# A hybrid decoder trunk on one core: gate products of the linear attention issued ahead, the first blocks of the feed-forwards' second matrix three products later, five slots in the last feed-forward

## The chip, the cores and the metric

One core of a Trainium2 chip runs the whole program as one launch. The metric is the device time of that core in microseconds (us), taken as the median of several executions; the time before the change is 2344.31 us (three executions, 2343.51 to 2345.34). TensorE is the matrix engine; VectorE (DVE), ScalarE (ACT) and GpSimd (POOL) are the three engines for element-wise work; SyncE (SP) issues most DMAs.

## The reference

One inference step of a two-layer decoder for 512 prompt tokens and 8 x 4 sample tokens, 544 in all, with 1024 features. Each layer is feed-forward, mixer, feed-forward; the first layer's mixer is a gated linear attention, the second's an attention with forget gates.

```
h += 1/2 gate0 * SwiGLU(adaLN0(h));  h += gate1 * Mixer(adaLN1(h));  h += 1/2 gate2 * SwiGLU(adaLN2(h))

def swiglu(u, w_up, w_down):                 # 1024 -> 2 x 2816 -> 1024
    a, b = jnp.split(u @ w_up, 2, axis=-1)
    return (jax.nn.silu(a) * b) @ w_down

def gla_mixer(u, s0, w_in, w_gate2, b_gate, g_out, w_out):
    q, k, v, r, glr = jnp.split(u @ w_in, ...)            # 4 heads, keys 128, values 256 wide
    log_a = jax.nn.log_sigmoid(glr @ w_gate2 + b_gate) / 16
    o, S = gla_chunk_scan(q * 128 ** -0.5, k, v, log_a, s0)   # decay = exp(cumsum(log_a))
    return (rmsnorm(o, g_out) * jax.nn.silu(r)) @ w_out, S
```

Outputs are the new activations, the keys, values and forget values, and the recurrent states.

## The kernel before

Everything is kept feature-major: `h` and the input `u` of each product lie as 128 partitions x 8 blocks x 544 tokens. Each float32 product is made of three matrix products in a short format: an operand is split into a rounded part (`hi`, a cast on ScalarE) and the rest (`lo`, a subtraction on VectorE). `halves` does both, and line 157 (ScalarE) and line 158 (VectorE) are its two instructions; `acc3` (lines 176 to 178) does the three matrix products. The 544 tokens are worked on in two halves of 272 columns.

**Order.** The program text is a list by priority. A planner issues it: it goes through the text with its own estimate of each instruction's cost, and gives each engine the earliest instruction of the text that it takes to be ready. The result is one fixed queue for each engine; at run time an engine that waits for one instruction does not go past it. Tiles with the same tag share a few buffers; a tile's first writer waits until a buffer is free.

**Feed-forward (`ffn_seven`).** It is used four times, under the names 00, 02, 10 and 12. The 2816 middle features are 22 blocks, `q`. Blocks 0 to 2 are multiplied in the plain way (`plain_up`: 24 matmuls for each of two matrices and each half). From block 3 on, `seven` does the up-product with a seven-product scheme over the two halves of the depth and of the tokens: products 1, 2, 6, 7, 5, 4, 3, in this order, of 12 matmuls each. It needs sums of input blocks: `inputs` makes T1, T2 and T4 from uh and ul by additions and subtractions on VectorE (lines 549 and 556) followed by `halves`, and `last_input` writes T3 over a quarter of uh and ul that is read no more after the plain blocks. Product 7 reads T3. With `late=True` the two sums that T3 needs are made a second time in `last_input`; with `late=False` a tile `t3` of 4 x 272 numbers for each partition keeps them, and `last_input` is one cast and one subtraction, 1088 wide. `stage` makes the weights' sums of the next block (POOL, lines 649 to 656) and splits them.

The blocks are grouped into rounds, (0,1,2), (3,4,5), ..., (18 to 21). While the products of round r run, the second matrix is applied to round r-1: 16 down blocks (`down_block`; 8 output blocks x 2 halves, 9 matmuls each, then `residual` on VectorE, lines 408 and 411). `down_weights(r, m2)` loads and splits the weights for two output blocks (`rd`, then `hd` and `ld`, 768 wide). `between`, called after each product, decides how many down blocks are issued by then: 16 are spread evenly over `n = min(7 * len(round), 7 * (slots - 3))` products, where `slots` is the number of buffers for the middle features (`gh`, `gl`). With 6 slots n is 21, with 5 slots 14. 00 and 02 have `slots=5, late=True`, 10 has 6 slots and keeps `t3`, 12 has 6 slots and `late=True`. In 00 and 02 `between` also ticks off small products for the modulation vectors (`ada`); in 12 it ticks off the update of the sample states (`state_start`, then 16 `state_step`).

**Linear attention (`gla`).** After the first q and k features come the token-major products for v in three chunks (`proj_steps`; five units for each chunk: token tiles 0 and 1, the samples, token tiles 2 and 3). The chunk with the gate's input `glr` is first. Then `glr` is transposed to gT, and eight small products `z` (`gate_half`; four heads, two halves) are evaluated: `Abs` on ScalarE (line 1143) and a minimum on VectorE (line 1144). `gate_logs` does `Exp` and `Ln` over all heads at once (lines 1147 and 1148), and `gate_sums(hd)` a subtraction and a running sum for one head (lines 1151 and 1152). In the text the first three units of chunk `v0` stand before, among and behind the eight `gate_half`; the last two of them stand behind `gate_sums(0)`, and `ahead(5)` prepares the next weights. For each head, seven levels follow: differences of the running sum (lines 1213 and 1214), `Exp` (line 1215), products with q and k (lines 1216 and 1217), small matmuls `at` (line 1225), and evacuation. After each level `fill(FL[...])` issues so many units of the remaining q, k and r features.

## Time and profile before

| | |
|---|---|
| median of three executions | 2344.31 us |
| the profiled execution | 2349.15 us |
| its span, first to last instruction | 2347.4 us |
| granted TensorE clock, mean | 0.988 |
| feed-forward 00, from the first plain block to the end | about 31 to 447 us |
| linear attention | about 440 to 735 us |
| feed-forward 02 | about 735 to 1165 us |
| feed-forward 10 | about 1281 to 1655 us |
| feed-forward 12 | about 1950 to 2347 us |

The profiled execution is 4.84 us above the median, of which 1.75 us lie outside its span. In the rows of a timeline the columns are: start and length in us, engine, line, operation, what is written from what, shape and number of instructions, and in brackets how long the engine had been idle and for whom it waited. In the list of waits the columns are: total in us, how often, and the longest.

### The profile page before, as it was taken

The numbers are of one execution on the slowest core, as the hardware profiler recorded it, in microseconds if no ns is written. First come the engines' busy times: TensorE is split into PE (matmuls) and PEld (weight loads), VectorE is DVE, ScalarE is ACT, GpSimd is POOL, SyncE is SP. The second block draws the span as 40 slices with busy tenths as digits, with TensorE's granted clock in tenths as the row PEclk, the third lists the DMA queues.
The fourth block names the chain that finished last, engine by engine and source line by source line (L and its number), as shares of the span: only waits on it lengthen the run. The fifth ranks groups of instructions, "written<-read, shape, count | busy, mean of one in ns | idle before, by whom it ended". The sixth has DMA issues, their size and how long they took to land.

```text
span 2347.4 us, 48948 instructions
## 1 busy us (share of the span) xinstructions
PE 2279.5 (97%) x19292; PEld 2128.8 (91%) x19292; DVE 1743.9 (74%) x3796; ACT 978.6 (42%) x1818; POOL 897.7 (38%) x908
## 2 busy tenths in 40 slices
PE   7999999998989999999999999999998999999999
PEld 6899999997979999999879999999895589999999
DVE  6877667738555976777685977787948758979885
ACT  3343333434533443333334444444446544434432
POOL 0344544206202354554210455652325122555551
PEclk8999999999999999999999999999999999999999
DMA  8545555422253426555448233333256641334441
GB/s 307 182 126 189 192 196 186 120 62 65 61 181 97 137 89 196 172 191 182 162 127 242 79 97 91 105 89 97 69 115 199 185 137 44 97 91 130 141 144 70
DMA packets 363035, 319.43 MB, mean 136 GB/s; under 512 B 25247, under 2 KB 326141, under 8 KB 362758
## 3 DMA queue, kind: packets, MB, share of 16 engines
q1 hardware_dynamic: 350182, 308.63, 41.8%
q0 software_dynamic: 12624, 7.67, 1.7%
q8 instruction: 152, 2.49, 0.4%
q14 instruction: 77, 0.63, 0.1%
HBM read 298.17 MB, written 18.38 MB: 135 GB/s over the span
## 4 chain that ended last, share of the span: by engine, by line
PE 80%; DVE 11%; DMA 3%; ACT 2%; issue 1%; POOL 1%; SPq 1%; DVEq 0%; ACTq 0%; POOLq 0%
PE p L176 11%; PE p L178 11%; PE p L177 11%; PE pd L177 7%; PE pd L178 7%; PE pd L176 7%; PE ada L242 2%; DVE nv L382 1%; DVE x L556 1%; PE fo L1835 1%; DVE lu L158 1%; PE pT L1820 1%; DVE ul L402 1%; PE fg L176 1%; PE fg L178 1%
## 5 line engine op out<-in xcount | busy, mean ns | idle before, releaser
L178 PE MATMUL pd<-gh,ld 128*128 128x272 f32 x1408 | 406.2, 288 | 4.3 <-DVE ld L158 4.3
L176 PE MATMUL pd<-gh,hd 128*128 128x272 f32 x1408 | 406.7, 289 | 3.3 <-DVE u L681 2.0
L177 PE MATMUL pd<-gl,hd 128*128 128x272 f32 x1408 | 406.3, 289 | 1.2 <-DVE gl L158 0.7
L176 PE MATMUL p<-uh,hu 128*128 128x272 f32 x1216 | 351.5, 289 | 0.0
L178 PE MATMUL p<-uh,lu 128*128 128x272 f32 x1216 | 350.7, 288 | 0.0
L177 PE MATMUL p<-ul,hu 128*128 128x272 f32 x1216 | 350.3, 288 | 0.0
L178 PEld LDWEIGHTS pd<-gh,ld 128*128 128x128 f32 x1408 | 265.6, 189 | 4.9 <-DVE ld L158 4.9
L176 PEld LDWEIGHTS pd<-gh,hd 128*128 128x128 f32 x1408 | 265.6, 189 | 4.2 <-DVE u L681 2.2
L177 PEld LDWEIGHTS pd<-gl,hd 128*128 128x128 f32 x1408 | 265.6, 189 | 2.2 <-DVE gl L158 0.9
L176 PE MATMUL p<-th,hu 128*128 128x272 f32 x912 | 264.9, 291 | 0.0
L178 PE MATMUL p<-th,lu 128*128 128x272 f32 x912 | 264.2, 290 | 0.0
L177 PE MATMUL p<-tl,hu 128*128 128x272 f32 x912 | 263.6, 289 | 0.0
L408 DVE SCALAR_TENSOR_TENSOR h<-pd,mods,h 128x272 f32<-128x272 f32 (+1 forms) x448 | 212.0, 477 | 65.9 <-PE pd L178 64.2
L158 DVE TENSOR_TENSOR lu<-rua,hu 128x512 fp32r<-128x512 f32 (+1 forms) x228 | 232.3, 1019 | 36.0 <-ACT hu L157 33.0
L157 ACT CAST hu<-rua 128x512 fp32r<-128x512 f32 (+1 forms) x228 | 173.8, 762 | 175.9 <-PE p L177 103.9
L176 PEld LDWEIGHTS p<-uh,hu 128*128 128x128 f32 x1216 | 229.0, 188 | 5.5 <-issue 2.9
L649 POOL TENSOR_TENSOR s<-rua,rub 128x512 f32<-128x512 f32 x76 | 121.5, 1599 | 290.9 <-DMA rub<-in_w_ffn_up_dram 161.7
L177 PEld LDWEIGHTS p<-ul,hu 128*128 128x128 f32 x1216 | 229.2, 189 | 0.1
L178 PEld LDWEIGHTS p<-uh,lu 128*128 128x128 f32 x1216 | 228.9, 188 | 0.0
L413 POOL TENSOR_TENSOR h<-h,gs 128x32 f32<-128x32 f32 x224 | 114.9, 513 | 239.4 <-DVE gs L411 223.3
L655 POOL TENSOR_TENSOR rua<-rub,rua 128x512 f32<-128x512 f32 x76 | 109.4, 1439 | 183.1 <-DVE lu L158 101.6
L176 PEld LDWEIGHTS p<-th,hu 128*128 128x128 f32 x912 | 172.7, 189 | 4.9 <-issue 2.1
(541 smaller groups left out, 5938.5 us busy)
## 6 DMA issues: line engine op xcount, KB each, us to landing
adaw<-in_w_ada_dram SPq DMA_DIRECT2D x128, 512.0 KB, 6.0
rua<-in_w_ffn_up_dram SPq DMA_DIRECT2D x88, 512.0 KB, 4.3
rub<-in_w_ffn_up_dram SPq DMA_DIRECT2D x88, 512.0 KB, 3.8
rd<-in_w_ffn_down_dram SPq DMA_DIRECT2D x96, 384.0 KB, 3.3
adah<-in_w_ada_dram SPq DMA_DIRECT2D x16, 512.0 KB, 5.9
adaw<-in_w_ada_kv_dram SPq DMA_DIRECT2D x16, 512.0 KB, 6.7
rd<-in_w_ffn_down_dram SPq DMA_DIRECT2D x16, 512.0 KB, 3.5
kp<-in_cache_k_dram SPq DMA_DIRECT2D x16, 512.0 KB, 10.7
```

Of the source, the lines that this page charges most:

```text
L157: S.copy(hi, src)
L158: V.tensor_tensor(out=lo, in0=src, in1=hi.bitcast(F32), op=ALU.subtract)
L176: PE.matmul(ps, lhsT=wh, rhs=xh, start=first and i == 0, stop=False)
L177: PE.matmul(ps, lhsT=wh, rhs=xl, start=False, stop=False)
L178: PE.matmul(ps, lhsT=wl, rhs=xh, start=False, stop=last and i == n - 1)
L242: PE.matmul(ps[32 * j:32 * j + 32, 0:256], lhsT=sc[:, k, :], rhs=t[:, j * 256:(j + 1) * 256], start=k == 0, stop=k == NB - 1)
L382: V.scalar_tensor_tensor(out=v[:, 0:p1 - t0], in0=h[:, k, t0:p1], scalar=mods[:, scale + k, 0:1], in1=rb[:, t0:p1], op0=ALU.mult, op1=ALU. ...
L402: V.scalar_tensor_tensor(out=ul[:, k, t0:p1], in0=v[:, :n], scalar=mods[:, shift + k, 0:1], in1=uh[:, k, t0:p1].bitcast(F32), op0=ALU.add, ...
L408: V.scalar_tensor_tensor(out=h[:, m, t0:p1], in0=ps[:, 0:n], scalar=mods[:, gate + m, 0:1], in1=h[:, m, t0:p1], op0=ALU.mult, op1=ALU.add)
L413: G.tensor_tensor(out=h[:, m, TP:T], in0=h[:, m, TP:T], in1=st[:], op=ALU.add)
L649: G.tensor_tensor(out=o["s3"][:], in0=a11, in1=a21, op=ALU.subtract)
L655: G.tensor_tensor(out=a11, in0=a21, in1=a11, op=ALU.subtract)
```

## The change

Three edits. In the linear attention all eight `gate_half` stand ahead of the units of `v0`; the logarithms are computed for head 0 and for heads 1 to 3 in separate instructions; three units of `v0` follow `gate_sums(0)`, and the last two are issued after the first and the second level of head 0, where `ahead(5)` now stands too; the row of `FL` for head 0 keeps its four units and has them later. In the feed-forwards the counter of `between` starts at -3 in the first round (`LAG`), so that the 16 down blocks of blocks 0 to 2 start three products later and are spread over three fewer; their first weights are loaded and split after the second product instead of ahead of the first. In the last feed-forward (12) `late=True` is taken away and there are five slots.

```diff
-FL = [1, 0, 1, 0, 1, 0, 1] + [0, 1, 0, 1, 0, 1, 1] * 3
+FL = [0, 0, 1, 1, 0, 1, 1] + [0, 1, 0, 1, 0, 1, 1] * 3
+LAG = 3
...
-            down_weights(0, 0)
             load(plain + 1)
             for r in range(1, len(rounds)):
                 todo = blocks(r - 1)
-                n, done, gone = min(7 * len(rounds[r]), 7 * (slots - 3)), [0], [0]
+                n, done, gone = min(7 * len(rounds[r]), 7 * (slots - 3)), [0 if r > 1 else -LAG], [0]
+                if r == 1:
+                    n -= LAG
                 def between():
                     done[0] += 1
+                    if r == 1 and done[0] == 2 - LAG:
+                        down_weights(0, 0)
                     while gone[0] < min(2 * NB * done[0] // n, 2 * NB):
...
-                S.activation(e1, e1, AF.Exp, scale=-1.0)
-                S.activation(e1, e1, AF.Ln, bias=1.0)
+                for func, scale, bias in ((AF.Exp, -1.0, 0.0), (AF.Ln, 1.0, 1.0)):
+                    for e in (e1[:, 0:1], e1[:, 1:4]):
+                        S.activation(e, e, func, scale=scale, bias=bias)
...
-            zs = [(hd, half) for hd in range(4) for half in range(2)]
-            for i in range(3):
-                v0[i]()
-                for _ in range((3, 3, 2)[i]):
-                    gate_half(*zs.pop(0))
+            for hd in range(4):
+                for half in range(2):
+                    gate_half(hd, half)
             gate_logs()
             gate_sums(0)
-            for s_ in v0[3:]:
+            for s_ in v0[:3]:
                 s_()
-            ahead(5)
+            v0 = v0[3:]
...
+                    if v0:
+                        v0.pop(0)()
+                        if not v0:
+                            ahead(5)
                     fill(FL[7 * hd + li])
...
-                  final=True, late=True)
+                  final=True, slots=5)
```

## The prediction

> **What bounds the kernel now.** I read the page's busy times first, then the list of TensorE's waits, then the timelines around the longest of them.

> ```profile
> PE 2279.5 (97%) x19292; PEld 2128.8 (91%) x19292; DVE 1743.9 (74%) x3796; ACT 978.6 (42%) x1818; POOL 897.7 (38%) x908
> ...
> PE at L1225 <- POOL xb L1217: 6.1, 3, 4.2
> ...
> PE pd L178 <- DVE ld L158: 4.3, 3, 2.4
> ```

> TensorE is busy 97% of the span, so an edit that keeps the matmuls can only gain idle time of TensorE, and slow matmuls. The longest waits touched by the edits are those for line 1217 (linear attention) and for `ld`, the split of the second matrix. The timeline of TensorE shows each with its place; I take the feed-forwards first (00, 02, 12 in this order).

> ```profile
> 85.83 0.39 PE L178 MATMUL pd<-gh,ld 128*128 128x272 f32 x1 [1.38 <-DVE ld L158]
> ...
> 90.57 0.39 PE L176 MATMUL pd<-gh,hd 128*128 128x272 f32 x1 [1.33 <-ACT gh L157]
> 91.70 0.59 PE L177 MATMUL pd<-gl,hd 128*128 128x272 f32 x1 [0.73 <-DVE gl L158]
> ...
> 799.15 0.39 PE L178 MATMUL pd<-gh,ld 128*128 128x272 f32 x1 [0.48 <-DVE ld L158]
> ...
> 2000.07 0.60 PE L178 MATMUL pd<-gh,ld 128*128 128x272 f32 x1 [2.40 <-DVE ld L158]
> 2000.46 0.43 PE L176 MATMUL pd<-gh,hd 128*128 128x272 f32 x1
> 2000.69 0.43 PE L177 MATMUL pd<-gl,hd 128*128 128x272 f32 x1
> ...
> 2127.24 0.39 PE L176 MATMUL pd<-gh,hd 128*128 128x272 f32 x1 [1.97 <-DVE u L681]
> ```

> The first down blocks wait 1.38 + 1.33 + 0.73 = 3.44 us in 00, 0.48 in 02 and 2.40 in 12; in 10 nothing waits there. After the 2.40 the matmuls start 0.23 us apart. In the linear attention:

> ```profile
> 528.58 0.29 PE L176 MATMUL gq<-uh,hgq 128*128 128x272 f32 x1
> ...
> 531.97 0.29 PE L176 MATMUL gq<-uh,hgq 128*128 128x272 f32 x1
> 532.09 0.29 PE L177 MATMUL gq<-ul,hgq 128*128 128x272 f32 x1
> 536.53 1.12 PE L1225 MATMUL at<-xb 128*64 128x64 f32 x8 [4.16 <-POOL xb L1217]
> ...
> 538.20 0.43 PE L177 MATMUL gq<-ul,hgq 128*128 128x272 f32 x1
> 538.43 0.43 PE L178 MATMUL gq<-uh,lgq 128*128 128x272 f32 x1
> ```

> v0 is done at 528.58, where the first q feature starts. The first `at` then stands at the head of TensorE's queue for 4.16 us. Matmuls of the same shape start 0.12 us apart ahead of it and 0.23 behind it, for about 15 of them: 15 x 0.11 = 1.6 us more. In 12 some 12 slow ones behind the 2.40 make 1.3 us.

> [...]

> **The change, part by part.**

> *Gate products ahead.* What the first `at` waits for is a chain over four engines.

> ```profile
> 510.27 1.18 PE L1142 MATMUL z<-kk,w 16*128 16x272 f32 x4
> ...
> 512.38 0.72 PE L1142 MATMUL z<-kk,w 16*128 16x272 f32 x2
> ...
> 507.28 0.18 DVE L1135 COPY kk<-glrT 16x32 f32<-16x32 f32 x1 [0.17 <-PE glrT L1134]
> ...
> 520.42 0.95 ACT L1143 ACTIVATE rr<-z,vec 128x272 f32<-128x272 f32 x2 [1.05 <-PE z L1142]
> ...
> 522.68 2.02 ACT L1147 ACTIVATE rr<-rr 128x2176 f32<-128x2176 f32 x1
> 524.60 1.03 ACT L157 CAST hgq<-rgq 128x1024 fp32r<-128x1024 f32 x1
> ...
> 526.95 2.03 ACT L1148 ACTIVATE rr<-rr 128x2176 f32<-128x2176 f32 x1
> ...
> 529.00 1.36 DVE L1151 TENSOR_TENSOR rr<-rr 128x544 f32<-128x544 f32 x2 [2.11 <-ACT rr L1148]
> 530.28 2.47 DVE L1152 TENSOR_TENSOR_SCAN bb<-kk,rr 128x544 f32<-128x544 f32 x2
> ```

> gT is complete at 507.28 + 0.18 = 507.5, and yet the last Abs ends at 520.42 + 0.95 = 521.4, since the products stand between units of v0. Issued first, a pair follows a pair after 512.38 - 510.27 = 2.1 us (two buffers, each freed by Abs and minimum): four pairs start at 507.5, 509.6, 511.7 and 513.8, and the last Abs ends some 1.7 later, at 515.5. From the last Abs to the first `at` it is 536.53 - 521.4 = 15.1 us now. Of these go: the cast `hgq` (1.03), which stands between Exp and Ln and moves behind v0; the second head's subtraction and scan (1.36/2 + 2.47/2 = 1.9), which the queue has between head 0's scan and its levels and which now wait for the second Ln; and Ln over four heads, of which only head 0 is left on the chain. No row has a 544-wide Exp or Ln. A line through 0.475 us for 272 columns (the Abs) and 2.02 for 2176 gives 0.70 for 544 and 1.58 for 1632; so Exp, Exp, Ln cost 2.98 where 4.05 stood, 1.1 less, and the two added instructions cost ScalarE about 0.5, half of it off the chain. 15.1 - 1.0 - 1.9 - 1.1 = 11.1: `at` is ready at 526.6. v0 keeps TensorE busy until 528.6. The work covers the chain by 2 us, and the four feature units stay for the later levels.

> So 4.16 + 1.6 = 5.8 can go. I book 4.7, since the last two units are behind the first two levels in priority, and the planner may put `at` ahead of matmuls that were ready: 1.1 stay. Bounds: all 5.8 and the smaller level waits too, 6.1 - 4.2 = 1.9 by the list's row (7.7 together); against the change, `at` in the queue directly behind v0's third unit, which would end near 521 (two units of 24 matmuls, 0.12 x 352/272 = 0.16 us each, sooner than 528.6): 526.6 - 521 = 5.6 of waiting instead of 4.16, a loss of 1.5.

> What is moved along: `ahead(5)` and its DMA come some units later. Its weights are first read after the third level, and its `hi` and `lo` buffers come free with v0's last unit; if the cast (1.03) and split come late, the first q feature waits for about 2 us that `at` work would then cover only in part. That lies within the 1.1 kept back and the bounds.

> *Down blocks three products later.* TensorE's matmuls are the same. What follows product 2 is now product 6 and product 7, with block 0 as the fifth thing instead of the second. So product 7, with T3, is wanted up to three blocks (27 matmuls of 0.125 us = 3.4 us) sooner, and the first `ld` three products (36 matmuls, 4.5 us) later. VectorE decides:

> ```profile
> 85.69 2.98 DVE L158 TENSOR_TENSOR ul<-x,uh 128x272 fp32r<-128x272 f32 x2
> ...
> 90.34 0.94 DVE L158 TENSOR_TENSOR ld<-rd,hd 128x768 fp32r<-128x768 f32 x1
> ...
> 92.83 0.44 DVE L158 TENSOR_TENSOR ul<-x,uh 128x272 fp32r<-128x272 f32 x1
> ...
> 803.41 0.43 DVE L158 TENSOR_TENSOR ul<-x,uh 128x272 fp32r<-128x272 f32 x1
> ...
> 1320.94 1.29 DVE L549 TENSOR_TENSOR ul<-t,uh 128x1088 fp32r<-128x1088 f32 x1 [0.33 <-ACT uh L582]
> ...
> 1972.99 1.14 DVE L556 TENSOR_TENSOR x<-uh,ul 128x272 f32<-128x272 f32 x3
> ...
> 1998.00 2.02 DVE L158 TENSOR_TENSOR ld<-rd,hd 128x768 fp32r<-128x768 f32 x1
> ...
> 2005.71 0.77 DVE L158 TENSOR_TENSOR ul<-x,uh 128x272 fp32r<-128x272 f32 x1
> ```

> In 00 T3 is complete at 92.83 + 0.44 = 93.3. Two `ld` (0.94 each) and a residual that stood before it go behind it: 90.9. Product 1 and two block matmuls had ended at 85.83 - 1.38 = 84.45, so product 7 comes at 84.2 + 2 x 1.5 = 87.2 and reads its last part of T3 at 88.3: a wait of 2.6 instead of 3.44. Then `ld` is split while product 7 runs. I book 0.7, between 3.44 (all of it; the planner puts product 5, which needs no T3, in between) and -1.0 (`ld` late too). In 02 T3 ends at 803.84, less the same two splits 801.0 to 802.0, and product 7 reads its last part at 802.5: in time. I book 0.4 of 0.48, with -0.8 for an `ld` that is late. In 10 TensorE waits for nothing there; the slack that shrinks by 3.4 us costs, I take, 0.2 (0 to 0.5). The second edge is SP's queue: `rd` now goes behind the next block's two loads, and takes a later buffer; the loads are 10 us ahead of their use, and I book nothing.

> That 16 blocks come in 11 products (00, 02, 12) or 18 (10): each block costs VectorE less than it costs TensorE (9 x 0.125 = 1.1 us), so a denser mixture leaves it no later. Nothing booked.

> *`t3` in 12.* Twelve additions and subtractions (1.14/3 = 0.38 each) go and four stay: -3.0; four `ul` (0.43) become one of 1.29: -0.4. T3 was complete at 2005.71 + 0.77 = 2006.5; less 3.4 and less `ld` (2.02) it is 2001.1. Product 2 had ended at 2000.07 - 2.40 - 0.25 = 1997.4; product 6 ends at 1998.9 and product 7 reads its last part at 2000.0: a wait of 1.1 to 1.2 in place of 2.40. A wait of that length has no slow matmuls behind it (85.83), so 1.2 + 1.3 = 2.5 booked, between 0 and 3.7.

> *Five slots in 12.* All 16 blocks of a round stand in 14 of its 21 products, and seven run alone.

> ```profile
> 944.00:956.00 12.00, 12.00 (x113) 10.91 (x112) 10.40 (x17) 4.77 (x9) 9.66 (x8) 1.00 0.62 215
> ...
> 2148.00:2160.00 12.00, 12.00 (x98) 12.00 (x98) 11.80 (x20) 5.24 (x10) 10.08 (x10) 1.00 0.57 171
> ```

> These are 12 us of 02 (five slots, no down block) and of 12 with state steps: VectorE works 10.40 and 11.80 of them (fifth column) and TensorE does not wait. Together they would be more than full, so I book 0.4 of loss, between 0 and 3. The 1.97 at 2127.24 falls in the state's start; its place among blocks changes, and I leave it, with 2 either way.

> **Sum** against the profiled execution of 2349.15: -4.7 - 0.7 - 0.4 + 0.2 - 2.5 + 0.4 = -7.7, so 2341.4; that execution stands 4.84 above the median, and 2344.31 - 7.7 = 2336.6.

> **The rivals.**

> *Everything goes.* All waits named vanish with the smaller ones: 7.7 + 3.44 + 0.48 + 3.7 + 1.97 = 17.3, so 2327.0; half of what I hold back gives about 2332. For it: the waits are single ones.

> *The queue freezes the wait.* The planner set `at` 4 us too early; if it errs by the same amount in the new order, the 5.8 stay with ready matmuls behind them. -7.7 + 4.7 = -3.0: 2341.3. For it: ready q matmuls stood behind the waiting `at` at 536.53 already. Against: a chain without the second head's scan.

> *VectorE and POOL.* Two `ul` took 2.98 where others take 0.44 each; the next block's POOL sums, whose loads are no longer behind `rd`, can fall on T3's steps. A freeze of 2.1 in each of 00, 02 and 12 takes what was booked there (3.6): 2340.2. [...]

> *Slower: five slots.* In the seven products alone (10.5 us) VectorE needs 10.5 x 10.40/12 = 9.1 at least, 11.80/12 of it or more with state steps. If one freeze of 2.1 and 1.5 of overload fall in each of four rounds and reach TensorE, that is 14.4: 2336.2 + 14.4 = 2350.6. It decides from about 13 us on. Against: five PSUM banks stand between the two engines.

> **How the numbers follow.** 0.2% (4.7 us) is about what a measurement here can tell. Chances: my sum 0.44 (its own range 2333 to 2339.5), everything goes 0.12, frozen queue 0.22, VectorE and POOL 0.14, five slots 0.08. Faster takes the first two and 0.10 of the next two, near the edge at 2339.6: 0.66. Same 0.27, slower 0.07. The range 2330 to 2343.5 leaves out the ends of the first rival and of the last.

> **What the profile would show.** Right: no wait over 1.5 us at line 1225 with v0's matmuls running up to it, the Abs rows done by 516; `at` first near 527; no `ld` wait in 12; T3 in 12 complete some 5 us sooner than now, counted from product 1. Wrong: an `at` wait of 4 us with gv matmuls behind it; product 7 waiting for `ul` or `uh`; new waits on VectorE every 50 us in the last feed-forward.

## Result: slower, and the profile after

The changed kernel takes 2360.57 us (median of five executions, 2355.89 to 2365.09) against 2343.51 for the kernel before in the same comparison: a ratio of 1.0071, 95% interval 1.0054 to 1.0089. I had forecast 2336.6, a gain. The profiled execution took 2365.09 (span 2363.3).

The page's busy times and the list of TensorE's waits (in us: total, times, longest) of the changed kernel:

```profile
PE 2291.6 (97%) x19292; PEld 2136.9 (90%) x19292; DVE 1742.8 (74%) x3785; ACT 978.7 (41%) x1819; POOL 900.7 (38%) x908
```

```profile
PE p L177 <- ACT uh L158: 6.5, 4, 2.1
...
PE pd L177 <- ACT gh L687: 4.1, 3, 2.3
...
PE p L178 <- DVE ul L159: 2.8, 5, 1.1
...
PE pd L178 <- POOL gl L688: 1.8, 3, 0.9
...
PE p L178 <- DVE tl L159: 1.6, 1, 1.6
```

The 6.1 us of `at` and the 4.3 of `pd` waiting for `ld` are gone from the list. In their place products (`p`) wait for `uh` and `ul`, which is T3, and in one place for `tl`, the last part of T2; down blocks (`pd`) wait for `gh` and `gl`. TensorE's timeline gives the places: product 7 in 00 and in 02, product 6 (`tl`) and product 7 (`ul`) in 12, then two of the seams in 12, the places where one round ends and the next begins.

```profile
88.68 0.40 PE L178 MATMUL p<-ul,hu 128*128 128x272 f32 x1 [1.10 <-DVE ul L159]
90.12 0.40 PE L178 MATMUL p<-ul,hu 128*128 128x272 f32 x1 [0.79 <-DVE ul L159]
92.69 0.60 PE L177 MATMUL p<-uh,hu 128*128 128x272 f32 x1 [2.06 <-ACT uh L158]
95.32 0.59 PE L177 MATMUL p<-uh,hu 128*128 128x272 f32 x1 [1.20 <-ACT uh L158]
...
801.28 0.39 PE L177 MATMUL p<-uh,hu 128*128 128x272 f32 x1 [1.72 <-ACT uh L158]
...
2006.17 0.48 PE L178 MATMUL p<-tl,hu 128*128 128x272 f32 x1 [1.59 <-DVE tl L159]
2008.07 0.59 PE L178 MATMUL p<-ul,hu 128*128 128x272 f32 x1 [0.97 <-DVE ul L550]
...
2160.97 0.39 PE L177 MATMUL pd<-gh,hd 128*128 128x272 f32 x1 [2.32 <-ACT gh L687]
...
2267.81 0.39 PE L177 MATMUL pd<-gh,hd 128*128 128x272 f32 x1 [1.52 <-ACT gh L687]
2269.10 0.58 PE L178 MATMUL pd<-gl,hd 128*128 128x272 f32 x1 [0.90 <-POOL gl L688]
```

To see what each place cost, waits, slow matmuls and all, I compare where the same matmul starts in the profile of a kernel and in the profile before. The difference of two such shifts, at the two ends of a stretch, is what the stretch lost (+) or gained (-). In the table, "booked" is the prediction, "after" the changed kernel, and the other columns are runs described below. The points in brackets are times of the kernel before, chosen where both have done the same blocks.

| Stretch | booked | after | gates alone | later blocks alone | slots and T3 alone |
|---|---|---|---|---|---|
| 00, first round (82 to 138) | -0.7 | +4.4 | -0.2 | +4.0 | -1.4 |
| linear attention (505 to 620) | -4.7 | -8.4 | -8.7 | -1.2 | -1.6 |
| 02, first round (766 to 837) | -0.4 | +5.9 | +0.1 | +6.4 | 0.0 |
| 10, first round (1305 to 1384) | +0.2 | +0.3 | +0.3 | +1.2 | +0.3 |
| 12, first round (1994 to 2048) | -2.5 | +1.4 | 0.0 | +3.5 | -2.1 |
| 12, rounds 2 and 3 (2048 to 2150) | 0 | -1.3 | 0.0 | 0.0 | -1.4 |
| 12, round 4 to the end (2150 to 2326) | +0.4 | +10.2 | 0.0 | -0.2 | +9.5 |

The seven stretches give +12.5 of the 15.9 us between the two profiles; the other 3.4 us lie outside them, where no edit reaches directly. There, too, a stretch differs by up to about 2 us from one profile to another: -2.1 to +1.2 in the linear attention, over the kernels without the gate edit. In the first round of 00, six of the nine kernels that leave it as it was show -1.4 to -1.6 and three -0.2 to 0.0.

So the gates gained more than booked, and two things that were booked at next to nothing (a gain of 0.9 for the later blocks, a loss of 0.4 for five slots) lost some 25 us between them: 15 by the later blocks alone, 9.5 to 10 by five slots. What made T3 late in 00 is in VectorE's and GpSimd's timelines:

```profile
84.27 1.42 DVE L550 TENSOR_TENSOR x<-x,x 128x272 f32<-128x272 f32 x1
85.72 1.42 DVE L557 TENSOR_TENSOR x<-uh,ul 128x272 f32<-128x272 f32 x1
87.06 1.21 DVE L159 TENSOR_TENSOR lu<-rua,hu 128x1024 fp32r<-128x1024 f32 x1
88.20 1.86 DVE L159 TENSOR_TENSOR ul<-x,uh 128x272 fp32r<-128x272 f32 x2
89.98 1.50 DVE L557 TENSOR_TENSOR x<-uh,ul 128x272 f32<-128x272 f32 x1
...
93.52 0.95 DVE L159 TENSOR_TENSOR ld<-rd,hd 128x768 fp32r<-128x768 f32 x1
...
94.74 0.43 DVE L682 TENSOR_TENSOR a<-p,u 128x272 f32<-128x272 f32 x1
95.09 0.68 DVE L159 TENSOR_TENSOR lu<-s,hu 128x512 fp32r<-128x512 f32 x1
95.69 0.43 DVE L159 TENSOR_TENSOR ul<-x,uh 128x272 fp32r<-128x272 f32 x1
```

```profile
81.95 3.44 POOL L650 TENSOR_TENSOR s<-rua,rub 128x512 f32<-128x512 f32 x1 [5.66 <-DVE g L623]
85.47 1.37 POOL L651 TENSOR_TENSOR rub<-rub 128x512 f32<-128x512 f32 x1
88.41 1.35 POOL L656 TENSOR_TENSOR rua<-rub,rua 128x512 f32<-128x512 f32 x1 [1.57 <-issue]
89.84 1.35 POOL L657 TENSOR_TENSOR rua<-rua 128x512 f32<-128x512 f32 x1
```

T3 is complete at 95.69 + 0.43 = 96.1. The third row is the split of the *next* block's weights (`stage` step 1); it now stands ahead of T3's last steps, and the sums at lines 656 and 657, which wait for it, run beside them. In the kernel before, the same split came behind T3 (complete at 93.3):

```profile
93.78 1.23 DVE L158 TENSOR_TENSOR lu<-rua,hu 128x1024 fp32r<-128x1024 f32 x1 [0.16 <-ACT hu L157]
```

Operations of 0.43 us take 1.42 to 1.50 while GpSimd adds. The first two slow `x` run beside the sums at lines 650 and 651 (step 0), which now come 3 us sooner (81.95 instead of 84.91); the load of one of their inputs is issued at 73.4 instead of 81.1, since it now goes ahead of `rd`. Product 7 waits 5.4 us for T3 in all (with one more wait of 0.26), where I had forecast 2.6.

### The profile page after: what moved, and what is told of

It is laid out like the page before. It is cut to its first block, busy times and chain, and to the rows that moved or that the text cites. A ratio compares the mean times of both kernels' runs of the same rounds, so it can differ in the third digit from the quotient of the medians.

```text
span 2363.3 us, 48925 instructions
## 1 busy us (share of the span) xinstructions
PE 2291.6 (97%) x19292; PEld 2136.9 (90%) x19292; DVE 1742.8 (74%) x3785; ACT 978.7 (41%) x1819; POOL 900.7 (38%) x908
## 4 chain that ended last, share of the span: by engine, by line
PE 77%; DVE 13%; DMA 4%; ACT 2%; issue 2%; POOL 2%; SPq 1%; ACTq 0%; DVEq 0%; POOLq 0%
PE p L177 11%; PE p L178 10%; PE p L179 10%; PE pd L178 7%; PE pd L177 7%; PE pd L179 7%; PE ada L243 2%; DVE lu L159 2%; DVE x L557 1%; DVE x L550 1%; DMA kp<-in_cache_k_dram 1%; DVE nv L383 1%; PE fo L1843 1%; DVE tl L159 1%; PE pT L1828 1%
## 5 line engine op out<-in xcount | busy, mean ns | idle before, releaser
L177 PE MATMUL pd<-gh,hd 128*128 128x272 f32 x1408 | 408.4, 290 | 4.1 <-ACT gh L687 4.1
L178 PE MATMUL pd<-gl,hd 128*128 128x272 f32 x1408 | 407.4, 289 | 1.9 <-POOL gl L688 1.8
L177 PE MATMUL p<-uh,hu 128*128 128x272 f32 x1216 | 353.3, 291 | 6.5 <-ACT uh L158 6.5
L178 PE MATMUL p<-ul,hu 128*128 128x272 f32 x1216 | 353.0, 290 | 4.1 <-DVE ul L159 2.8
L177 PEld LDWEIGHTS pd<-gh,hd 128*128 128x128 f32 x1408 | 267.1, 190 | 5.1 <-ACT gh L687 4.7
L178 PEld LDWEIGHTS pd<-gl,hd 128*128 128x128 f32 x1408 | 267.1, 190 | 3.0 <-POOL gl L688 2.7
L177 PE MATMUL p<-th,hu 128*128 128x272 f32 x912 | 265.3, 291 | 0.8 <-DVE gs L412 0.8
L178 PE MATMUL p<-tl,hu 128*128 128x272 f32 x912 | 263.5, 289 | 1.6 <-DVE tl L159 1.6
L158 ACT CAST hu<-rua 128x512 fp32r<-128x512 f32 (+1 forms) x228 | 173.8, 762 | 195.8 <-PE p L178 128.2
L177 PEld LDWEIGHTS p<-uh,hu 128*128 128x128 f32 x1216 | 230.6, 190 | 12.8 <-ACT uh L158 7.5
L178 PEld LDWEIGHTS p<-ul,hu 128*128 128x128 f32 x1216 | 230.7, 190 | 6.1 <-DVE ul L159 4.3
L177 PEld LDWEIGHTS p<-th,hu 128*128 128x128 f32 x912 | 172.9, 190 | 6.1 <-issue 2.5
```

Of the source, the lines that this page charges most:

```text
L158: S.copy(hi, src)
L177: PE.matmul(ps, lhsT=wh, rhs=xh, start=first and i == 0, stop=False)
L178: PE.matmul(ps, lhsT=wh, rhs=xl, start=False, stop=False)
```

## The experiments

All times are medians; each ratio is against the kernel before in the same comparison (its median was 2345.3 to 2345.9), with its 95% interval. The ratio is not the quotient of the two medians, and where the executions lie unevenly the two differ.

**The three edits by themselves.**

Gates alone (the hunks of the change's diff in `FL` and `gla`):

> The gate edit alone (all eight gate products first, logarithms in two parts, v0's last two units inside head 0), on the kernel before. Theory (the parts add up): TensorE reaches the first feature of the output projection 8 us sooner, since the 4.16 us wait for the first `at`, its slow matmuls and the small level waits are filled by v0's units: 2335.5, between 2333 and 2338. Rival (the gain seen in the linear attention of the changed kernel belongs partly to the 4 us by which it was late there): 2340 or more.

Measured 2339.16, ratio 0.9972 (0.9957 to 0.9986): a clear gain. The time is 1.2 us above the expected range and below the rival's 2340; the kernel before was slower, too, in this comparison (2345.67 instead of 2344.31), and the ratio applied to 2344.31 gives 2337.7, at the upper edge of the range. The later blocks alone (the hunks with `LAG` and `down_weights`):

> The later first blocks alone (counter from -3 in the first round of each feed-forward, first weights after product 2), on the kernel before. Theory (T3 is late): product 7 is wanted up to three blocks sooner and waits for the four last casts and subtractions of T3 in 00, 02 and 12; about +4.5 in 00, +6 in 02, +1 in 10 and +4 in 12, where T3 still is made the long way: 2359, between 2354 and 2363. Rival (the loss at the starts comes from the second matrix's weights or from the 11-product packing): the waits in the list are for `ld` or stand at blocks, and not at product 7.

Measured 2359.34, ratio 1.0056 (1.0035 to 1.0077), as expected. Five slots and the T3 tile alone (the last hunk, `late=True` to `slots=5`):

> The last edit alone (feed-forward 12 with t3 and five slots), on the kernel before. Theory (seams): the first block of a round follows product 1 instead of product 2, straight after seven products in which VectorE and POOL are full, and waits for the last middle block's gh and gl; about 9 us lost over rounds 3 to 6, 2 to 3 gained at the start of 12 through t3 and 1.5 at the state's start: 2348, between 2345 and 2352. Rival (the loss in 12 comes from the later first blocks, and five slots are harmless): 2339 to 2342.

Measured 2350.6, ratio 1.0021 (1.0008 to 1.0033), as expected. The parts add up to +0.5%, against +0.71% together; the intervals allow that. The table above shows the same by place.

**Why T3 is late.** In the first block of the seven-product scheme, steps 1 and 2 of the next block's staging are issued behind product 5 (with `LAG = 3`, nothing else changed):

```diff
                 a0 = plus_ps(q, "a0", ...)
-                stage(q + 1, 1)
+                if q != plain: stage(q + 1, 1)
...
-                stage(q + 1, 2)                 # behind product 7
+                if q != plain: stage(q + 1, 2)
...
                 u4 = plus_ps(q, "a4", p5, u2)
+                if q == plain: stage(q + 1, 1); stage(q + 1, 2)
```

> The later down blocks alone, with one more edit: in the first product block after the plain ones, steps 1 and 2 of the next block's staging are issued behind product 5 instead of behind products 2 and 7, which in the queue puts lu of that block (1.21 us on VectorE) and the two POOL sums that wait for it behind the last part of T3. Theory A (T3 is late because the next block's staging and the POOL sums behind it were queued ahead of its last parts; they cost lu 1.21 and two freezes of 1.1 in each of the feed-forwards 00, 02 and 12): 2349 to 2353, 6 to 10 us under the 2359.3 of the later blocks alone, with product 7's waits in 00 down from 5.4 to about 2.6. Rival B (product 7 is simply wanted 3.4 us sooner than T3 can be there; the staging fills time that is free): 2356 or more.

Measured 2352.65, ratio 1.0029 (1.0014 to 1.0043): inside theory A's range, 6.7 us less than the later blocks alone, and product 7's waits in 00 are 3.0 us instead of 5.4. VectorE and GpSimd in 00, of this run:

```profile
87.69 0.78 DVE L159 TENSOR_TENSOR ul<-x,uh 128x272 fp32r<-128x272 f32 x2
88.39 0.78 DVE L557 TENSOR_TENSOR x<-uh,ul 128x272 f32<-128x272 f32 x2
...
93.06 0.43 DVE L159 TENSOR_TENSOR ul<-x,uh 128x272 fp32r<-128x272 f32 x1
...
93.76 1.21 DVE L159 TENSOR_TENSOR lu<-rua,hu 128x1024 fp32r<-128x1024 f32 x1
```

```profile
95.11 1.28 POOL L656 TENSOR_TENSOR rua<-rub,rua 128x512 f32<-128x512 f32 x1 [7.65 <-issue]
```

T3 is complete at 93.5, `lu` and the sums come behind it, and the two `ul` take 0.78 instead of 1.86. (The two `x` beside step 0's sums still take 1.42 each.) The first round of 00 now loses 1.3 us instead of 4.0 and that of 02 1.4 instead of 6.4. In 12 nothing was gained (3.9). ScalarE's timeline there:

```profile
2006.08 0.62 ACT L158 CAST hu<-rua 128x512 fp32r<-128x512 f32 x1 [4.56 <-POOL rua L656]
2006.61 0.41 ACT L158 CAST uh<-x 128x272 fp32r<-128x272 f32 x1
```

The cast `uh`, a part of T3, stood behind a staging cast that waited 4.56 us for GpSimd's sum: the same staging, in another queue. That this is the whole cause in 12 is read from the rows and was not tested by a run.

What is left is that product 7 is wanted early. With product 5 ahead of product 7 in that block as well:

```diff
+                if q == plain: p5 = product(q, 5, o["S1"], T1)
                 u3 = plus_ps(q, "u3", product(q, 7, o["S3"], T3), u2)
...
-                p5 = product(q, 5, o["S1"], T1)
+                if q != plain: p5 = product(q, 5, o["S1"], T1)
```

> As the run before, and in that one block product 5, which needs no T3, comes ahead of product 7 (1.5 us of TensorE work between product 6 and product 7). Theory A: the rest of the wait in 00, 02 and 12 falls by 1.5 us each, and the slow matmuls behind it go: 2344 to 2349. Rival B: product 5's two evictions (0.43 each) and its own needs only move the wait: within 2 us of the run before.

Measured 2352.66, ratio 1.0028 (1.0013 to 1.0044), no better as a whole: by the time it is rival B's answer. By place, 00 turned from +1.3 to -2.0 and 02 from +1.4 to -0.1; 12 lost 5.1 instead of 3.9. These would make 3.6 us less in all, which the median does not show. So theory A fits the one trace in 00 and 02 and not in 12. Of the 2.0 in 00, 1.5 also appear in most kernels that leave 00 alone.

**Where five slots lose.** Five slots without the T3 tile:

```diff
-                  final=True, late=True)
+                  final=True, late=True, slots=5)
```

> Five slots in the last feed-forward alone, without the T3 tile (the quarter sums are computed again as before). If the loss is in the seams between rounds (the first block of a round comes one product sooner and waits for gh and gl of the last middle block), the seams cost their 9.6 us as they did with both edits, and the 3 us that the T3 tile saved at the start are missing: 2352 to 2355. Rival (the T3 tile itself costs, in VectorE's or SBUF's order): 2346 or less.

Measured 2354.96, ratio 1.0024 (1.0007 to 1.0041): as expected, the seams lose 9.8 us (round 4 to the end) without the tile, too, and the first round's gain is missing. Then the blocks moved two products back in rounds 2 to 6 of 12, with five slots and the tile:

```diff
-                n, done, gone = min(7 * len(rounds[r]), 7 * (slots - 3)), [0], [0]
+                d = 2 if r > 1 and name == "12" else 0
+                n, done, gone = min(7 * len(rounds[r]), 7 * (slots - 3)) - d, [-d], [0]
```

> As the run with five slots and t3 alone, but in 12 the counter of rounds 2 to 6 starts at -2, so that the first block of a round comes after product 3, and 16 blocks take 12 products. Theory A (the place of the first block: it is issued before the last middle block's chain of Silu, product, cast and POOL subtraction is done): the waits for gh and gl at the seams go, some 7 us less than with five slots alone: 2340. Theory B (VectorE is overloaded in the products without blocks, wherever they lie): nine products without blocks instead of seven leave it later still: 2348 or more, with waits at products or at the blocks.

Measured 2346.43, ratio 0.9999 (0.9984 to 1.0014). Neither answer: round 4 to the end still loses 5.2. So, again with five slots and the tile, I spread the 16 blocks of a round in 12 over 19 products, by taking the output tile only ahead of its first write:

```diff
-                g_tiles(q)                      # at the start of seven(q), in 12
...
+                if q not in gt: g_tiles(q)      # behind product 4
                 low(q, t0, t1, c21)
...
-                n = min(7 * len(rounds[r]), 7 * (slots - 3))
+                n = 7 * len(rounds[r]) - 2      # in 12
```

> Five slots and the T3 tile in the last feed-forward, with the loss in the seams aimed at: a middle block takes its output tile only ahead of its first write to it (behind product 4), so that the 16 blocks of a round spread over 19 of the 21 products and the first one stands behind product 2 again, as with six slots. Theory A (the loss of five slots is the first block of a round, one product sooner than gl of the last middle block): the seams' 9.6 us go, the T3 tile's 3 stay as a gain: 2341 to 2344, ratio 0.998 to 0.9995. Rival B (five slots hold VectorE's work back wherever the blocks stand; the wait moves to product 4 of the third middle block): 2347 or more.

Measured 2351.01, ratio 1.0014 (0.9997 to 1.003): theory A failed. The time is rival B's, but its wait at product 4 does not appear: TensorE waits 5.9 us for `gl` in six places, although the first block stands behind product 2 again. A row of its list of waits, and the timelines of TensorE and of GpSimd at one seam:

```profile
PE pd L177 <- POOL gl L687: 5.9, 6, 1.8
```

```profile
2158.20 0.39 PE L177 MATMUL pd<-gl,hd 128*128 128x272 f32 x1 [1.80 <-POOL gl L687]
```

```profile
2154.20 1.29 POOL L655 TENSOR_TENSOR rua<-rub,rua 128x512 f32<-128x512 f32 x1
2155.57 1.86 POOL L656 TENSOR_TENSOR rua<-rua 128x512 f32<-128x512 f32 x1
2157.40 0.75 POOL L687 TENSOR_TENSOR gl<-c,gh 128x272 fp32r<-128x272 f32 x1
```

The block that TensorE wants at 2156.4 needs `gl`, and `gl` stands in GpSimd's queue behind 3.2 us of sums for a block that is not wanted yet. That is a queue's order, not a place among products. The test is to take that one subtraction, for the last middle block of a round in 12, from GpSimd to VectorE:

```diff
-                (G if q not in rounds[-1] else V).tensor_tensor(out=lo, ...)
+                (G if q not in rounds[-1] and (name != "12" or all(q != x[-1] for x in rounds)) else V).tensor_tensor(out=lo, ...)
```

> As the run with the blocks of the last feed-forward spread over 19 products (2351.0), but in that feed-forward gl of the last middle block of each round is subtracted on VectorE instead of GpSimd. Theory A (gl stands in GpSimd's queue behind the next block's sums): TensorE's 5.9 us of waits for gl fall under 2, and the time to 2344 to 2348. Rival B (VectorE, 84% busy in the rounds, is what is late, and more work on it makes it later): 2349 or more.

Measured 2341.43, ratio 0.9984 (0.9965 to 1.0003). The median is 9.6 us less than in the run before, the ratio some 7 us, with about 6 either way: three of the twelve executions of the run before took 2340 to 2341 and the others 2348 to 2353. Its waits for the `gl` of line 687, in the list of waits:

```profile
PE pd L177 <- POOL gl L687: 0.4, 1, 0.4
PE pd L177 <- DVE gl L687: 0.2, 1, 0.2
```

5.9 us of waiting for the `gl` of line 687 have become 0.6, and round 4 to the end loses 0.4 instead of 4.6 (rounds 2 and 3: 1.0 instead of 2.5). The waits fell as theory A said, though the time came out below its range, and rival B is excluded: what was late is GpSimd's queue. In the traces it is worth 5.6 us. In the changed kernel itself, with the same one edit:

> The changed kernel with gl of the last middle block of each round of the last feed-forward on VectorE. Its seams cost 10.2 us in the trace. Theory A (the first block comes one product too soon, so that gh itself, 2.3 of the wait in the first seam, is late whichever engine makes gl): at most 4 us gained, 2356 to 2360. Rival B (GpSimd alone is late): 8 to 10 us gained, 2350 to 2353.

Measured 2353.45, ratio 1.0036 (1.0021 to 1.0051): about 7 us less than the changed kernel, between the two ranges and nearer to B's. The trace speaks for A:

```profile
PE pd L177 <- ACT gh L687: 4.2, 3, 2.3
```

This row stands as it did (4.1 us before the edit), the waits for `gl` fell only from 1.8 to 1.5, and round 4 to the end loses 7.6 instead of 10.2. Part of these 2.6 us may be half clock (last section): two stretches of 3.41 us follow the seams' waits in the changed kernel, and the mean granted clock of the profiled execution is 0.988 here and 0.983 there. The two medians are from different comparisons and each is uncertain by some 4 us, so how the 10 us of the changed kernel divide between a late `gh` and a late `gl` stays open.

**What gains in the gate edit.** All of v0 ahead of the levels:

```diff
-            for s_ in v0[:3]: s_()
-            v0 = v0[3:]
+            for s_ in v0: s_()
+            ahead(5)
...
-                    if v0: ...                  # one unit behind each level
```

> The gate edit alone, but with all of v0 run ahead of the score levels instead of one unit behind each level. If what helps is the earlier chain (gate products, logarithms of the first head, sum, scan), the first `at` is ready when v0 ends and the time is that of the gate edit, 2339 within 1.5. If what helps is v0's units as cover in the levels, the waits between levels come back (2.2 + 1.6 + 1.4 in the kernel before) and it is 2343 or more. In between (2341 to 2342.5): both.

Measured 2341.23, ratio 0.9977 (0.9962 to 0.9992). One pass for the logarithms, v0 as in the change:

```diff
-                for func, scale, bias in (...): for e in (e1[:, 0:1], e1[:, 1:4]): ...
+                S.activation(e1, e1, AF.Exp, scale=-1.0)
+                S.activation(e1, e1, AF.Ln, bias=1.0)
```

> The gate edit alone with the logarithms of all four heads in one pass, as they were, instead of the first head's ahead of the others'. Its part: exp of the first head ended at 510.3 and its ln at 513.1 in the gate edit's trace; in one pass they wait for all eight gate halves (516.5) and take 1.28 + 2.02 + 1.28 + 2.03, so the first `at` is ready about 10 us later, at 530, where TensorE has v0's last units to cover it in part. If the split carries the gain: 2342 or more. If the order of the gate products carries it: within 1.5 of 2339.2.

Measured 2340.29, ratio 0.9985 (0.9972 to 0.9997). The first lies where both reasons were to count, the second where the order of the gate products was to carry the gain; but the intervals of both overlap with that of the whole gate edit, so the times alone don't tell the three apart. The stretch 505 to 620 in the one trace of each reads otherwise: -8.7 for the whole edit (between -7.8 and -8.8 in all seven kernels that hold it), -3.6 without v0 among the levels, +0.1 with one pass, where kernels without the edit show -2.1 to +1.2. By the profiles both parts are needed, the split above all; the medians do not show that, and the profiled execution with one pass (2345.62) was one of the two slowest of its twelve. Which part carries the gain stays open.

**Versions that keep what gained.** The gate edit and the slots edit with 19 products (the run with 19 products is the "run before" of this text):

> The gate edit and the run before together, no later down blocks. If they add up: 2339.2 less 3, so 2335 to 2338.5. If the T3 tile's gain is lost again to VectorE's load: 2339 to 2341.

Measured 2341.6, ratio 0.9983 (0.9969 to 0.9997): nothing added. In 12 the tile's first round gains 3.6, and the seams lose 2.4 in rounds 2 and 3 and 3.8 from round 4 to the end; TensorE again waits 6.0 us for `gl`. With 00's later blocks, staging behind T3 and product 5 first:

> As the run before, and the later down blocks in the feed-forward 00 alone, with the staging behind T3 and product 5 ahead of product 7. In the run with product 5 first, 00 gained 2.05 us in the trace (02 0.1, while 10 and 12 did not gain): 1 to 3 us under the run before, 2333 to 2337. Rival: it is a difference of one trace, and nothing is left of it: the same as the run before within 1 us.

Measured 2337.63, ratio 0.9972 (0.9955 to 0.999). The same with `gl` on VectorE:

> The gate edit, the later down blocks in the feed-forward 00 with staging behind T3 and product 5 first, and five slots with the T3 tile, 19 products and gl on VectorE. If gl on VectorE mends the seams: 2331 to 2335. If not: 2337 to 2340, as without it (2337.6).

Measured 2334.72, ratio 0.996 (0.9946 to 0.9975), as expected: the lowest median, faster than both kernels, 26 us below the changed one, with all three ideas in it. The waits for `gl` fell from 4.8 to 0.5 and the loss from round 4 to the end from 4.1 to 0.4, the second time that this one subtraction does it. And the same with 12 as in the kernel before:

> The gate edit and the feed-forward 00 as in the run before, the last feed-forward as in the kernel before (six slots, no T3 tile). The gate edit measured 2339.2, 00 gains 2 in a trace: 2336 to 2338. If 00's gain is one trace's: 2339 to 2340.

Measured 2337.1, ratio 0.9966 (0.9952 to 0.9981). Whether five slots and the tile add anything to six slots (0.996 against 0.9966) the intervals leave open; they overlap with that of the gate edit alone (0.9972) as well.

## Why the prediction was wrong, point by point

**Gates: right mechanism, too small.** I had `at` ready at 526.6. It started at 526.17 without a wait in a kernel that was 4.4 us late by then, and at 520.12 in the gate edit alone:

```profile
526.17 0.68 PE L1229 MATMUL at<-xb 128*64 128x64 f32 x8
```

I had let all eight `Abs` go ahead of the logarithms. The planner put head 0's between them:

```profile
513.16 1.28 ACT L1154 ACT_TABLE_LOAD   x1
514.45 0.66 ACT L1154 ACTIVATE rr<-rr 128x544 f32<-128x544 f32 x1
515.01 0.85 ACT L1148 ACTIVATE rr<-z,vec 128x272 f32<-128x272 f32 x2
...
517.17 0.66 ACT L1154 ACTIVATE rr<-rr 128x544 f32<-128x544 f32 x1
```

The estimate of 0.70 for a 544-wide logarithm was right (0.66). The sum left out that the split by heads makes two more table loads, of 1.28 us each (first row; five between 500 and 535 us where three stood). The `q` weights that I feared would be late are: 1.07 and 1.76 us at the first q feature, 2.8 together where I feared about 2. The gain was 8.4, outside the bound of 7.7.

**Later blocks: the term that failed.** "T3 ... 90.9" was a subtraction of what leaves the queue, with everything else left where it was. 00's T3 came at 96.1. The 5.2 us between are, by the lengths of rows that nearly all stand above: `lu` 1.21; three `x` of 1.42, 1.42 and 1.50 instead of 0.43 (3.05); two `ul` in 1.86 instead of 0.78 (1.08); one `ld` that stayed ahead (0.95), a second `lu` (0.68) and an evicted product (0.43); less 2.2 of the old freeze (2.98 for two `ul`). When product 7 would want T3 I had right (87.2; it begins at 87.30). In 02, forecast "in time", the stretch lost 5.9; with the staging put back the 6.4 of the later blocks alone became 1.4 there. The rival *VectorE and POOL* named the mechanism, but as one freeze of 2.1 in each place, which would only have taken back what was booked there. For the loads' order I booked nothing. With it step 0's sums fall on T3's steps (two of the slow `x`, 2.0 us), which about replaces the old freeze; whether the order brought them there was not tested by itself. The run with the staging put back kept that order and lost most of the delay, so it is not the main part. What moved is the staging: the planner pulled it up once the blocks no longer stood ahead of it. The prediction's own sign of being wrong, product 7 waiting for `ul` or `uh`, is what the profile shows.

**T3 in 12.** The tile is worth more than the 2.5 booked: 3.3 between the runs with five slots with and without it (-2.1 against +1.2), 3.6 in the run with 19 products. But the later blocks cost 3.5 in the same place, and together it is +1.4. Product 7's wait came out near the forecast (0.97 for 1.1 to 1.2); what was left out is product 6, which waits 1.59 for `tl`, and 6.83 us in which the granted clock was 0.50, from 2006.32 on.

**Five slots: mis-sized from 0.4 to about 10.** I looked at VectorE's load in the seven products alone. The loss is at the seam: the first block of a round stands one product sooner, and what it reads hangs on VectorE, ScalarE and GpSimd in turn, each with a queue of staging and state steps ahead of it. The waits for `gh` and `gl` are 4.1 + 1.8 = 5.9 us, and the two stretches behind them, 3.41 us each at a granted clock of 0.50 (from 2163.33 and 2269.14 on), cost by my estimate half their length, 3.4, more. The rival *five slots* had the sign and roughly the size (14.4 against 10) for a loss that it put between the seams instead of at them. Its argument against, that five PSUM banks stand between the engines, does not bear on `gh` and `gl`, which lie in SBUF.

**The wait of 1.97 at the state's start** that I left in place is gone in the changed kernel (-1.3), within the 2 allowed; with five slots and 19 products it is there again (1.98 and 2.16, last section).

## What to carry to other kernels

When a planner fills queues from a priority list, taking work out from ahead of an instruction does not bring the instruction forward by that much: the next ready work of another kind moves in. Estimate the new queue, not the old one with holes in it, and look there for work that is not wanted yet (here the next block's staging), and price it with the slowdown of the engine beside it (here 0.43 us became 1.42 to 1.50). A consumer placed one product sooner should be priced by the chain that produces its operand, engine by engine; moving one subtraction to another queue took away waits of 5.3 us, where moving the first block back behind product 2 had left 5.9.

## What the runs showed of the hardware

VectorE was slower beside GpSimd than I priced: a 512-wide `lu` took 3.15 us in the changed kernel's round 4, where GpSimd was busy for 3.07 of them, and another 0.68 at 2159.44, where GpSimd did nothing.

```profile
2150.01 3.15 DVE L159 TENSOR_TENSOR lu<-s,hu 128x512 fp32r<-128x512 f32 x1
...
2159.44 0.68 DVE L159 TENSOR_TENSOR lu<-rua,hu 128x512 fp32r<-128x512 f32 x1
```

```profile
2151.32 1.29 POOL L656 TENSOR_TENSOR rua<-rub,rua 128x512 f32<-128x512 f32 x1
2152.69 1.62 POOL L657 TENSOR_TENSOR rua<-rua 128x512 f32<-128x512 f32 x1
```

The first ended only at 2153.16, with a `gl` subtraction (0.77 us from 2150.59 on), one whole sum of GpSimd (1.29) and a part of the next (1.62) inside it: here a single operation lasted beside more than one of the other engine.

In these traces matmuls started 0.23 us apart instead of 0.13 behind some waits of little over 2 us, and not behind others of nearly the same length. In the best version (first three rows) and the run with `gl` on VectorE (last three), at the state's start:

```profile
2113.26 0.39 PE L177 MATMUL pd<-gh,hd 128*128 128x272 f32 x1 [2.16 <-DVE u L682]
2114.74 0.43 PE L178 MATMUL p<-tl,hu 128*128 128x272 f32 x1
2114.96 0.43 PE L179 MATMUL p<-th,lu 128*128 128x272 f32 x1
```

```profile
2117.78 0.40 PE L176 MATMUL pd<-gh,hd 128*128 128x272 f32 x1 [1.98 <-DVE u L681]
2119.13 0.28 PE L177 MATMUL p<-tl,hu 128*128 128x272 f32 x1
2119.26 0.28 PE L178 MATMUL p<-th,lu 128*128 128x272 f32 x1
```

After 2.16 us the matmuls start 0.23 us apart from 1.2 us behind the wait on, for all 11 that begin by 2117; after 1.98 they stay at 0.13. The length of one wait alone does not tell the two apart: in the kernel before, the matmuls behind the waits of 1.33 and 0.73 (at 90.57 and 91.70) start 0.23 us apart, and those behind the 1.97 at 2127.24 do not.

In the prediction I took waits of 1.2 as free and those of 2.4 as costing 1.3 more; a sequence of waits, each below 2.1 us, as in 00 of the changed kernel, had 10.24 us at a clock of 0.50 in it (from 91.44 on), with 22 matmuls 0.23 us apart at its end.
